# Pool group maps behind the keys' sums of squares in a two-layer hybrid decoder

## The chip, the cores and the metric

The kernel runs on one core of a Trainium2 chip. The metric is the device time of one execution in microseconds. The times of before are the median of three runs; the trace is one more execution, taken with the hardware profiler. TensorE (PE) multiplies matrices, VectorE (DVE) and ScalarE (ACT) do elementwise work, GpSimd (POOL) does some of it too, and SyncE (SP) issues most transfers. Each engine works through its own queue in order.

## What is computed

Two decoder layers over 264 token columns (256 of a prompt, 8 of a sample group), each of an FFN, a mixer and a second FFN, with a layer norm behind each. The mixer is a gated delta rule (four heads, from q, k, v) beside a causal pooling of four channel groups. Cut to what matters here:

```python
def pool_mix(p, buf, start_pos, pool_w, pool_scale):
    ...
    for gi, w in enumerate(POOL_WINDOWS):            # 2, 4, 8, 16
        s = end[:, :, sl] - cs[:, POOL_BUF + 1 - w:POOL_BUF + 1 - w + L, sl]
        means.append(s / cnt[None, :, None])
    d = jnp.concatenate(means, axis=-1) - ext[:, POOL_BUF:]
    y = jnp.einsum('blgc,gcd->blgd', d, pool_w).reshape(B, L, POOL_DIM) * pool_scale

def mixer(h, ...):
    proj = h @ w_in
    qkv_c, new_conv = causal_conv(qkv, conv_buf, conv_w)
    k = l2norm(k.reshape(B, L, DN_HEADS, DN_HEAD_DIM))
    ...
    out = jnp.concatenate([o_dn, o_pool], axis=-1) @ w_out
```

## The kernel before, in words

Activations lie transposed: 128 channels on the partitions, 264 tokens along the row. Every large product is done in three float32r matmuls: high part of the weight by high and by low part of the activation, and low part of the weight by the high part (`mm3`, lines 221 to 223). A product over 1024 channels is thus 24 matmuls into one PSUM tile.

Weights come from memory in units of two pieces. `W.load` issues the transfer into one of three `wraw` buffers, ScalarE rounds each piece into its high part (`whi`, line 180), and VectorE subtracts to get the low part (`wlo`, line 185); some pieces go to tiles named `xhi` and `xlo`. There are three pairs of `whi` and `wlo`, so a piece can be split once the product three places ahead of it is done. `W.ahead(n)` asks for pieces until `n` are ready or on their way.

TensorE's order is the order of the program. On the other engines a scheduler chooses the order when the kernel is built, by priority: what is written earlier comes first, and what stands inside `tc.high_priority()` goes ahead of it. After that the order is fixed.

In the mixer the products go q0, p3, q1, p2, q2, p1, q3, p0, v0 to v3, z0 to z3. `q_tile`, `v_tile` and the keys' `conv` (line 526) make a causal convolution: one ScalarE instruction and three on VectorE (128x255, 128x254, 128x253) into tiles `c0` to `c11`, of which `c0` to `c3` are the keys, `c4` to `c7` q and `c8` to `c11` v. `p_tile(g)` copies the product of Pool group g into `ext`, and GpSimd adds up windows there: g + 1 additions into `wsum` (line 615), of which two buffers exist; `ext` has two as well. `p_map(g)` does two things. At its call VectorE makes the difference `dm` of window mean and token, in four instructions (lines 626, 628, 630, 631); the function that it returns issues the map itself later: the matmul `py` (line 635), a scaled copy `yp` (line 637), and the split of `yp` into high and low part. For groups 0 to 2 the differences have raised priority, for group 3 not:

```python
                with tc.high_priority() if g < 3 else nullcontext():
                    nc.vector.scalar_tensor_tensor(dm[:, 16:SEQ], cur[:, 31:15 + SEQ], 1.0 / wd, ext[:, 31:15 + SEQ],
                                                   ALU.mult, ALU.subtract)
                    ...
                def finish():
                    py = psa.tile([P, T], F32, name="py", tag="ax")
                    nc.tensor.matmul(py, pw[:, g, :], dm, start=True, stop=True)
```

Beside these runs the gate: a chain of some 25 small VectorE instructions of 128x12 (`s_`, `y_`, `p_`, `xa`, `gg`) with raised priority. It ends in four products `gm` (line 708, 128x512 each), which `pdiff` (line 718) sums on TensorE into the decays `DT`. `sumsq` (lines 735 to 743) transposes the keys on TensorE (`psq`), squares them on ScalarE and adds them up on VectorE; with `wsc` that scales the scores `MT` (line 762), which are computed between the matmuls of v3. `pP` transposes `MT`, and the solver follows.

The FFN's last stage makes eight tiles `pd`. Ahead of the last two, weights for six pieces are asked for when another layer part follows (`xnext`), else for four.

Of the kernel before, what the change touches and what calls it, by code (L numbers as in the profile page):

```python
# [18 lines left out]
KD = D // P  # L19
# [71 lines left out]
def trunk(ctx: ExitStack, tc: tile.TileContext, a: dict):  # L91
# [28 lines left out]
    def behind(ins):  # L120
        return nullcontext() if ins is None else tc.issue_after(ins.ins)

    def tables(name):
        tc.keep_in_program_order(nc.scalar.preload_act_table_set(name))
# [9 lines left out]
    def split(hi, lo, src):  # L134
        ins = nc.scalar.activation(hi, src, AF.Copy)
        nc.vector.tensor_sub(lo, src, hi.bitcast(F32))
        return ins
# [79 lines left out]
    W = Weights(units)  # L217

    def mm3(ps, w, k, xh, xl, first, last):
        hi, lo = w  # L220
        nc.tensor.matmul(ps, hi[:, k, :], xh, start=first, stop=False)  # L221
        nc.tensor.matmul(ps, hi[:, k, :], xl, start=False, stop=False)  # L222
        nc.tensor.matmul(ps, lo[:, k, :], xh, start=False, stop=last)  # L223

    def product(w, nm):
        ps = psm.tile([P, T], F32, name="p" + nm, tag="mm")
        for k in range(KD):
            mm3(ps, w, k, HH[:, k, :], HL[:, k, :], k == 0, k == KD - 1)
        return ps

    def two_products(nms):

        ws = [W.get() for _ in nms]
        ps = [psm.tile([P, T], F32, name="p" + nm, tag="mm") for nm in nms]
        for k in range(KD):
            for p, w in zip(ps, ws):
                mm3(p, w, k, HH[:, k, :], HL[:, k, :], k == 0, k == KD - 1)
        return ps
# [190 lines left out]
    def ffn(src, norm, xnext, late=False):  # L429
        with tc.tile_pool(name="fp", bufs=1, reuse_waits="tile") as fp:  # L430
            gh = [fp.tile([P, T], F32R, name=f"gh{m}") for m in range(KF)]
            gl = [fp.tile([P, T], F32R, name=f"gl{m}") for m in range(KF)]

            def gate(m, y, bias, u, ubias):
                sg = fp.tile([P, T], F32, name="sg", tag="sg", bufs=2)
                gt = fp.tile([P, T], F32, name="gt", tag="gt", bufs=2)
                if bias is None:
                    with behind(hi1 if src is None and m == 0 else None):
                        nc.scalar.activation(sg, y, AF.Silu)
                    nc.vector.tensor_mul(gt, sg, u)  # L440
                else:
                    nc.scalar.activation(sg, y, AF.Silu, bias=bias)
                    nc.vector.scalar_tensor_tensor(gt, u, ubias, sg, ALU.add, ALU.mult)
                split(gh[m], gl[m], gt)

            first = 0
            if src is not None:
                W.ahead(6)
                raw = src.raw_products("gugugu", [((0,), 0, 6), ((1,), 0, 6), ((2,), 0, 6), ((3,), 0, 6), None,
                                                  ((0, 1, 2, 3), 6, KD), ((4, 5), 0, KD)] if late else  # L450
                                                 [((0, 1), 0, 4), None, ((0, 1), 4, KD), ((2, 3), 0, KD), ((4, 5), 0, KD)])
                src.normalise()
                W.after, W.after_hi = src.y_op, src.exp_op
                tables("silu_and_others")
                W.ahead(2)
                W.after = W.after_hi = None

                ws = [W.get(), W.get()]
                ps = [psa.tile([P, T], F32, name="p" + nm, tag="ax") for nm in "gu"]
                for k in range(KD):  # L460
                    for p, w in zip(ps, ws):
                        mm3(p, w, k, HH[:, k, :], HL[:, k, :], k == 0, k == KD - 1)
                W.ahead(2)
                for m in range(3):
                    gate(m, *src.settle(raw[2 * m]), *src.settle(raw[2 * m + 1]))
                gate(3, ps[0], None, ps[1], None)
                first = 4
            for m in range(first, KF):
                W.ahead(4)
                if src is None and m == 4:  # L470
                    constants_in()
                if src is None and m == 0:
                    pg, pu = two_products("gu")
                else:
                    pg = product(W.get(), "g")
                    pu = product(W.get(), "u")
                gate(m, pg, None, pu, None)
            tables("natural_log_exp_and_others")
            w, i = None, 0
            for m in range(KD):  # L480
                W.ahead(6 if m > 5 and xnext else 4)
                if m > 2:
                    norm.before(m, 2.0 * ALPHA)
                ps = psm.tile([P, T], F32, name="pd", tag="mm")
                for k in range(KF):
                    if i % KD == 0:
                        w = W.get()
                    mm3(ps, w, i % KD, gh[k], gl[k], k == 0, k == KF - 1)
                    i += 1
                    if m == 2 and k == 10:  # L490
                        norm.shift2()
                        norm.before(m, 2.0 * ALPHA)
                norm.add_scaled(m, ps, 2.0 * ALPHA)


    def mixer(l, src, norm, xstack):
        with tc.tile_pool(name="mp", bufs=1, reuse_waits="tile") as mp:
# [32 lines left out]
            def silu(after):  # L530
                for c in silus:
                    with tc.issue_after(after.ins):
                        nc.scalar.activation(c, c, AF.Silu)
                silus.clear()
# [42 lines left out]
            def q_tile(j, ps=None):  # L577
                W.ahead(4)
                conv(ps or product(W.get(), "q"), 4 + j)
                cq[j] = ct[4 + j]  # L580
# [39 lines left out]
            def p_map(g):  # L620
                ext, smp, cur = pend[g]
                wd = 2 << g
                dm = mp.tile([P, T], F32, name="dm", tag="dm", bufs=2)
                csm = cur[:, 15 + SEQ:].rearrange("p (b i) -> p b i", i=16)
                with tc.high_priority() if g < 3 else nullcontext():
                    nc.vector.scalar_tensor_tensor(dm[:, 16:SEQ], cur[:, 31:15 + SEQ], 1.0 / wd, ext[:, 31:15 + SEQ],
                                                   ALU.mult, ALU.subtract)
                    nc.vector.scalar_tensor_tensor(dm[:, SEQ:], csm[:, :, 15], 1.0 / wd, smp[:, :, 15],
                                                   ALU.mult, ALU.subtract)
                    nc.vector.tensor_mul(dm[:, 0:16], cur[:, 15:31], cst[:, C_INV + 16 * g:C_INV + 16 * g + 16])  # L630
                    nc.vector.tensor_sub(dm[:, 0:16], dm[:, 0:16], ext[:, 15:31])
# [4 lines that stand above are left out]
                    yp = lpool.tile([P, T], F32, name="yp", tag="sq", bufs=4)  # L636
                    nc.scalar.activation(yp, py, AF.Copy, scale=sm[:, l, S_PS + g:S_PS + g + 1])
                    split(mh[4 + g], ml[4 + g], yp)

                return finish  # L640
# [50 lines left out]
            conv(kr[3], 3)  # L691
            ck = ct[0:4]
            map3 = p_map(3)
            p_tile(1)
            map3()
            q_tile(3)
            map2 = p_map(2)
            p_tile(0)

# [19 lines left out]
                e_last = nc.scalar.activation(DT[:, :, j * P:(j + 1) * P], pd, AF.Exp)  # L719
            tables("silu_and_others")  # L720
            silu(e_last)
            map2()
            v_tile(0, e_last)
            map1 = p_map(1)


            ssa = mp.tile([P, 2 * H + 2 * H * NB], F32, name="ssa")
# [17 lines left out]
            v_tile(1, e_last)  # L745
            for t in range(2):
                sumsq(ck, ssk, ke, t)
            map1()
            v_tile(2, e_last)
            wsc = mp.tile([P, 2, H], F32, name="wsc")  # L750
            with tc.high_priority():
                nc.vector.reciprocal(wsc, ssk)
                nc.vector.tensor_mul(wsc, wsc, beta[:, 0:2, :])
            map0 = p_map(0)
            norm.centre()

# [535 lines left out]
    def constants_in():  # L1292
        nc.sync.dma_start(out=sm, in_=a["small"])
        nc.sync.dma_start(out=cst, in_=a["cst"])
        nc.scalar.activation(onr, cst[:, C_M1024:C_M1024 + P], AF.Copy)
        nc.scalar.activation(far, cst[:, C_ID:C_ID + P], AF.Copy, scale=-FAR)
        nc.scalar.activation(gto, cst[:, C_ONE:C_ONE + 2 * P].rearrange("p (i n) -> p i n", i=2), AF.Copy)
        for t in (*parts, kq.bitcast(F32)):
            nc.gpsimd.memset(t, 0.0)
# [105 lines left out]
```

## Time and profile before

| | us |
|---|---|
| median of three runs | 1093.57 (1092.8 to 1093.61) |
| the profiled execution | 1093.62 |
| its span, first to last instruction | 1091.8 |
| TensorE busy | 1050.5 (96%) |
| VectorE busy | 751.9 (69%) |
| ScalarE busy | 596.9 (55%) |
| GpSimd busy | 158.2 (14%) |

The chain that ended last is TensorE for 87% of the span, VectorE for 5%, "issue" for 3% and ScalarE for 3%. Busy shares are means over stages with different limits, so the stretch of a mixer in which TensorE waits is read by itself: the first layer's lies between 222 and 275 us of the span, the second layer's 535.8 us later. A time in brackets at a row's end is the idle time of the engine ahead of that instruction, with what ended it.

### The profile page before, as it was taken

What the parts mean: (1) busy time and instruction counts of PE and PEld (TensorE: products, weight loads), DVE (VectorE), ACT (ScalarE), POOL (GpSimd) and SP (SyncE); (2) the same over time, 40 slices, a digit from 0 to 9 for tenths busy, and PEclk for the clock granted to TensorE, in tenths of its full rate; (3) what the DMA queues carried; (4) which work ended last, traced back from release to release, by engine and by line L of the source; (5) the groups of instructions that cost most, each with busy time, mean ns of one, the idle gap of its engine ahead of it and who ended that gap; (6) DMA issues with size and microseconds to landing.
All of it is one profiled execution on the core that took longest, in us unless ns stands there. A gap on an engine that the chain in (4) does not pass through costs nothing.

```text
span 1091.8 us, 20807 instructions
## 1 busy us (share of the span) xinstructions
PE 1050.5 (96%) x8434; PEld 1033.1 (95%) x8434; DVE 751.9 (69%) x1223; ACT 596.9 (55%) x1081; POOL 158.2 (14%) x206
## 2 busy tenths in 40 slices
PE   8999999969999999999999999999699999999995
PEld 8999999959889999999999999999598999999995
DVE  5555567896789965557785555778787898555554
ACT  6444445647947744454574444466388377444443
POOL 0000022232540000003200000322233300000031
PEclk9999999989999999999999999999899999999998
DMA  8554445732234355544625545565331344554541
GB/s 305 186 192 175 176 177 185 278 122 89 81 135 163 139 192 194 182 168 190 242 101 198 177 175 191 180 238 190 111 113 64 133 187 157 191 184 171 187 155 40
DMA packets 35840, 183.23 MB, mean 168 GB/s; under 512 B 6817, under 2 KB 12577, under 8 KB 15521
## 3 DMA queue, kind: packets, MB, share of 16 engines
q1 hardware_dynamic: 28672, 175.19, 44.1%
q10 hardware_dynamic: 7072, 6.72, 1.8%
q8 instruction: 66, 1.08, 0.4%
q14 instruction: 30, 0.24, 0.1%
HBM read 175.18 MB, written 6.72 MB: 167 GB/s over the span
## 4 chain that ended last, share of the span: by engine, by line
PE 87%; DVE 5%; issue 3%; ACT 3%; DMA 2%; SPq 0%; ACTq 0%; DVEq 0%
PE pd L221 7%; PE pd L223 7%; PE pd L222 7%; PE pu L223 7%; PE pu L222 7%; PE pu L221 7%; PE pg L222 7%; PE pg L221 7%; PE pg L223 7%; ACT S L896 1%; DVE xlo L185 1%; PE pop L221 1%; DMA wba<-in_w_ba 1%; PE pq L221 1%; PE pq L222 1%
## 5 line engine op out<-in xcount | busy, mean ns | idle before, releaser
L185 DVE TENSOR_TENSOR wlo<-wraw,whi 128x1024 fp32r<-128x1024 f32 (+1 forms) x301 | 367.1, 1223 | 206.3 <-ACT whi L180 205.9
L180 ACT ACTIVATE whi<-wraw 128x1024 fp32r<-128x1024 f32 (+1 forms) x301 | 312.4, 1041 | 329.7 <-issue 116.9
L221 PE MATMUL pd<-gh,whi 128*128 128x264 f32 x704 | 200.3, 285 | 0.0
L223 PE MATMUL pd<-gh,wlo 128*128 128x264 f32 x704 | 199.9, 284 | 0.0
L222 PE MATMUL pd<-gl,whi 128*128 128x264 f32 x704 | 198.8, 282 | 0.0
L221 PE MATMUL pg<-HH,whi 128*128 128x264 f32 x632 | 179.6, 284 | 0.9 <-ACT whi L180 0.9
L222 PE MATMUL pg<-HL,whi 128*128 128x264 f32 x632 | 179.4, 284 | 0.7 <-DVE HL L381 0.7
L223 PE MATMUL pu<-HH,wlo 128*128 128x264 f32 x632 | 179.2, 284 | 0.8 <-DVE wlo L185 0.8
L223 PE MATMUL pg<-HH,wlo 128*128 128x264 f32 x632 | 179.4, 284 | 0.5 <-DVE wlo L185 0.5
L221 PE MATMUL pu<-HH,whi 128*128 128x264 f32 x632 | 179.4, 284 | 0.0
L222 PE MATMUL pu<-HL,whi 128*128 128x264 f32 x632 | 179.1, 283 | 0.0
L222 PEld LDWEIGHTS pd<-gl,whi 128*128 128x128 f32 x704 | 132.5, 188 | 0.0
L223 PEld LDWEIGHTS pd<-gh,wlo 128*128 128x128 f32 x704 | 132.5, 188 | 0.0
L221 PEld LDWEIGHTS pd<-gh,whi 128*128 128x128 f32 x704 | 132.5, 188 | 0.0
L222 PEld LDWEIGHTS pg<-HL,whi 128*128 128x128 f32 x632 | 119.2, 189 | 1.2 <-DVE HL L381 1.2
L221 PEld LDWEIGHTS pg<-HH,whi 128*128 128x128 f32 x632 | 119.1, 188 | 1.1 <-ACT whi L180 1.1
L223 PEld LDWEIGHTS pu<-HH,wlo 128*128 128x128 f32 x632 | 118.6, 188 | 1.2 <-DVE wlo L185 1.2
L223 PEld LDWEIGHTS pg<-HH,wlo 128*128 128x128 f32 x632 | 118.6, 188 | 0.8 <-DVE wlo L185 0.8
L222 PEld LDWEIGHTS pu<-HL,whi 128*128 128x128 f32 x632 | 119.2, 189 | 0.0
L221 PEld LDWEIGHTS pu<-HH,whi 128*128 128x128 f32 x632 | 119.2, 189 | 0.0
L305 POOL TENSOR_TENSOR s<-X 128x264 fp32r<-128x264 f32 x4 | 3.0, 761 | 632.2 <-DVE X L302 632.2
L440 DVE TENSOR_TENSOR gt<-sg,pu 128x264 f32<-128x264 f32 x79 | 33.9, 429 | 50.4 <-PE pu L223 50.4
(374 smaller groups left out, 2013.1 us busy)
## 6 DMA issues: line engine op xcount, KB each, us to landing
wraw<-in_f_gu SPq DMA_DIRECT2D x86, 1024.0 KB, 4.8
wraw<-in_f_d SPq DMA_DIRECT2D x44, 1024.0 KB, 4.8
wraw<-in_w_in SPq DMA_DIRECT2D x20, 1024.0 KB, 4.9
wraw<-in_w_out SPq DMA_DIRECT2D x8, 1024.0 KB, 4.8
S<-in_sdelta SPq DMA_DIRECT2D x8, 512.0 KB, 6.5
out_o_ds<-S ACTq DMA_DIRECT2D x8, 512.0 KB, 2.6
X<-in_xT ACTq DMA_DIRECT2D x4, 264.0 KB, 5.6
out_o_y<-X SPq DMA_DIRECT2D x4, 264.0 KB, 2.4
```

The source lines that it names most:

```text
L180: self.last_hi = nc.scalar.activation(h, r, AF.Copy)
L185: nc.vector.tensor_sub(l, r, h.bitcast(F32))
L221: nc.tensor.matmul(ps, hi[:, k, :], xh, start=first, stop=False)
L222: nc.tensor.matmul(ps, hi[:, k, :], xl, start=False, stop=False)
L223: nc.tensor.matmul(ps, lo[:, k, :], xh, start=False, stop=last)
L305: nc.gpsimd.tensor_add(self.s2, X[:, 0, :], X[:, 1, :])
L440: nc.vector.tensor_mul(gt, sg, u)
L896: nc.scalar.activation(s, s, AF.Copy, scale=ab[:, h * NB + b:h * NB + b + 1])
```

## The change

Three things are changed.

The maps of groups 3 and 2 are issued behind the keys' sums of squares, no longer behind `p_tile(1)` and ahead of v0; that of group 1 follows v2 and the scale `wsc`; the differences of group 1 are called with the map of group 2 done. Group 0's map stays behind v3. The differences of group 3 get raised priority like the others'. And in an FFN that another part follows, six pieces are asked for ahead of the seventh tile only; behind the last tile four are asked for.

```diff
-                W.ahead(6 if m > 5 and xnext else 4)
+                W.ahead(6 if m == 6 and xnext else 4)
...
                 norm.add_scaled(m, ps, 2.0 * ALPHA)
+                if m == KD - 1 and xnext:
+                    W.ahead(4)
...
-                with tc.high_priority() if g < 3 else nullcontext():
+                with tc.high_priority():
                     nc.vector.scalar_tensor_tensor(dm[:, 16:SEQ], cur[:, 31:15 + SEQ], 1.0 / wd, ext[:, 31:15 + SEQ],
...
             map3 = p_map(3)
             p_tile(1)
-            map3()
             q_tile(3)
             map2 = p_map(2)
             p_tile(0)
...
             silu(e_last)
-            map2()
             v_tile(0, e_last)
-            map1 = p_map(1)
...
             for t in range(2):
                 sumsq(ck, ssk, ke, t)
-            map1()
+            map3()
+            map2()
+            map1 = p_map(1)
             v_tile(2, e_last)
...
                 nc.vector.tensor_mul(wsc, wsc, beta[:, 0:2, :])
+            map1()
             map0 = p_map(0)
```

The third part moves nothing: with it or without it the rows on all five engines follow in the same order, and only numbers of tiles differ.

On TensorE, between the product p1 (`pp`) and the product q3 (`pq`) of the first mixer:

```order
 L222 MATMUL pp<-HL,whi 128x264
 L223 MATMUL pp<-HH,wlo 128x264
-L635 MATMUL py<-dm,pw 128x264
 L221 MATMUL pq<-HH,whi 128x264
 L222 MATMUL pq<-HL,whi 128x264
```

The map of group 3 no longer stands there; it and the map of group 2 come behind the eight transposes `psq`, ahead of v2.

On VectorE before, from the last step of the key tile `c1` (`c_2785`) over the low part of p1, the `wlo` (`c_2828` and `c_2875` are the key tiles c2 and c3, `c_2779` is q1's):

```order
L526 SCALAR_TENSOR_TENSOR c_2785<-raw,sm,c_2785 128x253
L662 TENSOR_TENSOR s__2714<-s__2714,e__2713 128x12
L526 SCALAR_TENSOR_TENSOR c_2828<-raw,sm,c_2828 128x255
L663 TENSOR_TENSOR y__2715<-s__2714 128x12
L526 SCALAR_TENSOR_TENSOR c_2875<-raw,sm,c_2875 128x255
L664 TENSOR_SCALAR p__2716<-y__2715 128x12
L185 TENSOR_TENSOR wlo<-wraw,whi 128x1024
L666 SCALAR_TENSOR_TENSOR p__2716<-p__2716,y__2715 128x12
L526 SCALAR_TENSOR_TENSOR c_2779<-pq,sm,c_2779 128x255
```

And VectorE now, in the same place:

```order
L528 SCALAR_TENSOR_TENSOR c_2785<-raw,sm,c_2785 128x253
L628 SCALAR_TENSOR_TENSOR dm<-wsum,ext 128x240
L630 SCALAR_TENSOR_TENSOR dm<-wsum,ext 128x8
L632 TENSOR_TENSOR dm<-wsum,cst 128x16
L664 TENSOR_TENSOR s__2714<-s__2714,e__2713 128x12
L528 SCALAR_TENSOR_TENSOR c_2828<-raw,sm,c_2828 128x255
L633 TENSOR_TENSOR dm<-dm,ext 128x16
L665 TENSOR_TENSOR y__2715<-s__2714 128x12
L185 TENSOR_TENSOR wlo<-wraw,whi 128x1024
L666 TENSOR_SCALAR p__2716<-y__2715 128x12
L528 SCALAR_TENSOR_TENSOR c_2779<-pq,sm,c_2779 128x255
```

The four differences of group 3 have come up to a place ahead of the small gate instructions, and the first step of c3 has gone behind. From there to the next `wlo`, that of q3, there stand five convolution steps among small `p_` instructions, before and now.

On VectorE before, from the low part of p0, the next `wlo` but one, to the second pair of `gm` (`c_2869` is q2's tile):

```order
L185 TENSOR_TENSOR wlo<-wraw,whi 128x1024
L708 TENSOR_TENSOR gm<-cst,gp 128x512 x2
L676 TENSOR_TENSOR gp<-gg,gp 128x8
L682 TENSOR_TENSOR ad<-as__2744,cst 8x32
L526 SCALAR_TENSOR_TENSOR c_2869<-pq,sm,c_2869 128x255
L708 TENSOR_TENSOR gm<-cst,gp 128x512 x2
```

And now, from the same `wlo` to the first pair of `gm`:

```order
L185 TENSOR_TENSOR wlo<-wraw,whi 128x1024
L671 SCALAR_TENSOR_TENSOR xa<-p__2716,xa 128x12
L528 SCALAR_TENSOR_TENSOR c_2869<-pq,sm,c_2869 128x255
L673 TENSOR_TENSOR gg<-xa,nega 128x12
L528 SCALAR_TENSOR_TENSOR c_2875<-raw,sm,c_2875 128x254
L528 SCALAR_TENSOR_TENSOR c_2869<-pq,sm,c_2869 128x254
L528 SCALAR_TENSOR_TENSOR c_2875<-raw,sm,c_2875 128x253
L709 TENSOR_TENSOR gm<-cst,gp 128x512 x2
```

Ahead of these rows, behind the low part of q3, the four differences of group 2 and the first step of c3 now stand; before, one difference of group 3 stood there, and the `gm` came straight behind p0's low part. One more step of q2's tile now stands between the two pairs of `gm`: four convolution steps more in all ahead of the second pair. On SyncE the loads of `ext` for groups 1 and 0 go from behind two weight loads to ahead of one each.

## Rows read from the trace of the kernel before

**Rows 1.** Waits of TensorE: engine, line, releaser; us in total, times, longest
```profile
PE py L635 <- issue: 21.1, 2, 10.6
```

**Rows 2.** Chain that ended last in time, first layer: start, us, what
```profile
234.45 10.56 issue
245.01 1.22 PE py L635 x2
...
253.33 2.28 PE pdiff L718 x10
255.61 0.45 PE py L635 x2
...
272.30 0.87 PE pP L1027 x8
```

**Rows 3.** Timeline of TensorE: start, us, engine, line, out<-in
```profile
222.68 0.28 PE L221 MATMUL pq<-HH,whi 128*128 128x264 f32 x1
...
225.58 0.28 PE L221 MATMUL pp<-HH,whi 128*128 128x264 f32 x1
...
245.66 0.79 PE L221 MATMUL pq<-HH,whi 128*128 128x264 f32 x1
...
253.17 0.62 PE L718 MATMUL pdiff<-gm,gto 128*128 128x512 f32 x2
```

**Rows 4.** Windows: length, busy PE, PEld, DVE, ACT, POOL, granted clock, DMA share, GB/s
```profile
203.00:206.00 3.00, 1.59 (x10) 1.34 (x10) 2.44 (x6) 0.92 (x4) 2.48 (x5) 1.00 1.06 388
...
240.00:242.00 2.00, 0.00 (x0) 0.00 (x0) 2.00 (x7) 0.00 (x0) 0.40 (x1) 0.50 0.63 266
```

**Rows 5.** Timeline of VectorE
```profile
227.11 0.81 DVE L662 TENSOR_TENSOR s__2714<-s__2714,e__2713 128x12 f32<-128x12 f32 x1
...
228.23 0.98 DVE L663 TENSOR_TENSOR y__2715<-s__2714 128x12 f32<-128x12 f32 x1
229.13 0.47 DVE L526 SCALAR_TENSOR_TENSOR c<-raw,sm,c 128x255 f32<-128x255 f32 x1
229.53 0.16 DVE L664 TENSOR_SCALAR p__2716<-y__2715 128x12 f32<-128x12 f32 x1
229.60 1.21 DVE L185 TENSOR_TENSOR wlo<-wraw,whi 128x1024 fp32r<-128x1024 f32 x1
230.74 0.81 DVE L666 SCALAR_TENSOR_TENSOR p__2716<-p__2716,y__2715 128x12 f32<-128x12 f32 x1
...
233.84 1.21 DVE L185 TENSOR_TENSOR wlo<-wraw,whi 128x1024 fp32r<-128x1024 f32 x1
...
238.84 1.27 DVE L708 TENSOR_TENSOR gm<-cst,gp 128x512 fp32r<-128x512 f32 x2
...
244.25 0.41 DVE L626 SCALAR_TENSOR_TENSOR dm<-wsum,ext 128x240 f32<-128x240 f32 x1 [1.66 <-POOL wsum L615]
...
244.74 0.17 DVE L631 TENSOR_TENSOR dm<-dm,ext 128x16 f32<-128x16 f32 x1
```

**Rows 6.** Timeline of GpSimd
```profile
225.87 3.32 POOL L615 TENSOR_TENSOR wsum<-wsum 128x396 f32<-128x396 f32 x3
230.09 1.43 POOL L615 TENSOR_TENSOR wsum<-ext 128x398 f32<-128x398 f32 x1 [0.91 <-POOL wsum L615]
241.60 2.62 POOL L615 TENSOR_TENSOR wsum<-wsum 128x396 f32<-128x396 f32 x2 [10.07 <-DVE dm L630]
...
247.76 0.85 POOL L615 TENSOR_TENSOR wsum<-ext 128x398 f32<-128x398 f32 x1 [2.00 <-ACT ext L609]
```

**Rows 7.** Timeline of SyncE's issues
```profile
230.84 6.65 SPq L162 DMA_DIRECT2D wraw<-in_w_in  x2
244.99 1.01 SPq L604 DMA_DIRECT2D ext<-in_spool  x2
```

**Rows 8.** Timeline of ScalarE
```profile
264.69 0.54 ACT L637 ACTIVATE yp<-py,sm 128x264 f32<-128x264 f32 x1
```

**Rows 9.** The page's DMA issues: KB each, median us to landing
```profile
wraw<-in_w_in SPq DMA_DIRECT2D x20, 1024.0 KB, 4.9
```

## The prediction

> **What bounds the kernel now.** I read the waits by engine first, for TensorE, because it is busy for 96% of the span. One line stands out: the matmul of a Pool group map, `py`, has TensorE idle for 21.1 us in two waits, one in each layer [rows 1]. The chain of waits, read in order of time, puts the first at 234.45 and makes it 10.56 us long; nothing else on that chain is near it [rows 2]. The chain calls its cause "issue", so I looked for it in the instructions in order of time on VectorE and GpSimd. `py` reads `dm`, and the last of the four instructions that fill the `dm` of group 3 is the 128x16 subtraction at 244.74 [rows 5]; `py` starts 0.1 us behind its end. In VectorE's queue that subtraction stands behind the first difference of group 2 (244.25), which had waited 1.66 us for GpSimd's sums. Those sums had themselves waited 10.07 us for VectorE, for a `wsum` buffer that group 3's differences still held [rows 6]. So the two engines wait for each other in turn, and the start of the loop is that group 3's differences, without priority, were drawn to the end of VectorE's backlog.
>
> The stall costs more than its length. In the windows, TensorE's granted clock is 1.00 over a stretch with an idle time of 1.4 us (203 to 206) and 0.50 in 240 to 242, that is 1.2 of 2.4 GHz, after TensorE had stood still for 5 us [rows 4]. A product of 24 matmuls takes 2.90 us at full clock (222.68 to 225.58); the two products behind the stall take 253.17 - 245.66 = 7.51 us, which is 1.71 us more than 5.80 [rows 3]. The two matmuls of `py` take 0.65 us there (245.01 to 245.66) against 0.45 at full clock: another 0.20 [rows 2, 3].
>
> **The change part by part.** *The maps.* On TensorE the map of group 3 leaves its place between the products p1 and q3, and the map of group 2 its place behind `pdiff`; both now stand behind `psq`, and the map of group 1 follows v2. None is added, so the eight matmuls per layer cost the same. The wait goes whole, since nothing that the new places read is late there: the differences of groups 3 and 2 are done some 15 us earlier. Taken away per layer: 10.56 + 1.71 + 0.20 = 12.47 us. That is the ceiling, 24.9 us for the two layers.
>
> *What is late next.* TensorE needs the low parts of weights, which VectorE makes, and VectorE had a backlog at 234: the low part of q3 was made at 233.84 to 235.05 [rows 5], already later than q3's third matmul could now run (234.45 + 0.24 = 234.7). So I walk VectorE's new order with the durations of before.
>
> Step 1: up to the end of the c1 step (227.11) nothing moves. Then group 3's differences come, and they wait for GpSimd, whose three sums end at 225.87 + 3.32 = 229.19; with VectorE idle the last two take nearer 0.85 than 1.1 each [rows 6], so about 228.9. A new wait of 1.8 us, behind which stand the small gate instructions, a convolution step and the low part of p1. The four differences take 0.57 us (244.25 to 244.74 and one more step) [rows 5]. But in that stretch before, two 128x12 instructions took 0.81 and 0.98 us instead of 0.16, because GpSimd was at work, and they end with its sums [rows 5, 6]. They now run behind the sums: 1.47 us less, start to start. One convolution step, 0.40 us (229.13 to 229.53), moves behind. The low part of p1 starts at 229.60 + 1.8 + 0.57 - 1.47 - 0.40 = 230.1 and ends at 231.3, just in time for p1 at 225.58 + 2 x 2.90 = 231.4.
>
> Step 2: from there to the low part of q3 it took 233.84 - 229.60 = 4.24 us, with one hold by GpSimd of 0.65 in it (230.74). Now GpSimd does all three sums of group 2 in this stretch, since no buffer is missing. The three holds that rows show (0.81, 0.98 and 0.81 against 0.16) cost 0.71 in the mean, so three cost 2.1 and the stretch takes 4.24 - 0.65 + 2.1 = 5.7. The low part of q3 starts at 235.8 and, 1.21 long, ends at 237.0 [rows 5]. **TensorE waits for it 2.3 us**; without holds it would be 0.2, with a full 0.85 for each 2.8.
>
> The Trainium skill ("SBUF — State Buffer", Who interferes with whom) says that a VectorE instruction with two inputs in SBUF and a GpSimd instruction that reads SBUF share a port as a lock, and the loser stands for the whole instruction. The long 128x12 rows agree, as they end when GpSimd does. By the rule taken strictly each of the five sums of groups 2 and 1 holds VectorE for its 0.85 us, 4.25 in place of the 2.85 that I take here and in step 3; that would put 2.8 us more on the two layers, 1079 us.
>
> Step 3: from the low part of q3 to the `gm` product that `pdiff` needs second, before: 238.84 + 0.61 - 233.84 = 5.61 us. Added in the new order: group 2's differences 0.57 for the 0.32 of one of group 3's, four convolution steps 1.58, a small instruction 0.08, and holds by the two sums of group 1 between 0 and 1.5, of which I take 0.75. That is 8.3 us: the `gm` is there at 244.1. TensorE, with its wait of 2.3, would be at this matmul at 234.45 + 5.80 + 0.23 + 2.3 = 242.8. **A second wait of 1.3 us.** Behind it VectorE makes v0's and v1's low parts (1.14 each) while `pdiff` needs 2.28 [rows 2], so no third wait; convolution and the SiLUs of the keys are done before `psq`.
>
> Step 4: behind `psq` two maps in place of one put two more ScalarE instructions (0.54 us for the first [rows 8]) and one VectorE instruction between the squares and the scale of the scores. TensorE also has one map more to do there, 0.45 us, which it does not do elsewhere; so only 0.3 us per layer is left as a wait. Nothing in the later order looks worse than that.
>
> *Priority* is what makes step 1 possible: alone it would end most of the stall. *The weight parts behind the last FFN tile:* the order on all five engines is the same with and without it, apart from tile numbers, so 0; the 1.4 us of idle at 203 stay [rows 4]. *On SyncE* two loads of `ext` move in front of weight loads; see the last rival.
>
> **Sum.** Per layer 12.47 - 2.3 - 1.3 - 0.3 = 8.6 us, for two layers 17.2. The profiled execution took 1093.62 us (1.8 outside its span), 0.05 over the median of the runs, so no correction: 1093.6 - 17.2 = 1076.4; I say 1076. A change of 0.2%, 2 us, is about the least that a measurement of this kernel can tell.
>
> **Rivals.** *A, the holds do not come:* VectorE and GpSimd slip past each other. Step 2 then leaves 0.2 us and step 3 0.6, so 11.6 per layer, 1070. For it: convolution steps of 0.47 us stand between held rows, not held themselves. Against: every 128x12 instruction that met a running sum was held. 17%.
>
> *B, the queue runs later and the clock falls:* full holds of 0.85 give waits of 2.8 us at q3 and 2.0 at `pdiff`, and with 0.6 behind `psq` 7.1 per layer are left, 1079.4; if TensorE falls to 0.50 in them, 1.71 per layer is lost again: 1083. Against the clock part: it held 1.00 over the idle 1.4 us, and these are two waits with a product between them. The Trainium skill ("TensorE: Matmul & The Clock Gate", HAM oscillation) says that idle gaps send the clock back to half; no row here shows a gap of 2 to 3 us. 17%.
>
> *C, another wait takes the stall's whole place:* the maps leave, but VectorE's queue holds TensorE as long at q3 and `pdiff`, so within 2 us of 1093. For it: VectorE stood idle for only 1.66 us in the whole stall [rows 5], so its backlog is real. Against: it would have to hold TensorE for 12.5 us, and the waits that I can name, with full holds, come to 5.4. 3%.
>
> *D, slower:* SyncE. The load of v2's and v3's weights was issued at 230.84 [rows 7]. Now it stands behind an `ext` load that waits for group 3's last difference and the store of its tail (the two such loads of before were issued at 244.99, just behind those differences). In the walk that is 230, and the buffer for the weights comes free at 231.3, so nothing is lost. v2 starts at about 254 (`pdiff`, two products, `psq` and two maps behind 244.1); less 4.9 us to land [rows 9] and 2.3 to split, the load must be issued by 246.8. Beyond that each microsecond is lost, and only past 255.4 would a layer be slower than before. At 260, for example, that is 4.6 per layer, 1103. 2%.
>
> **How the numbers follow.** Forecast 60% (1073 to 1079.5), A 17%, B 17%, C 3%, D 2%, the rest beyond. A range of 1070 to 1082 takes in A's value, both ends of the holds and the first half of B, and leaves out some 15%. Faster by over 0.2% is the forecast with A and B and a part of C: 95%; within 0.2%: 2%; slower: 3%.
>
> **What would show it.** In the new profile: no wait of TensorE before `py`, clock 1.00 from 234 to 256. Step 1 is right if VectorE waits some 2 us for `wsum` before the first `dm`. Step 2: TensorE waits about 2 us for `wlo` at the third matmul of q3, 30 us behind the idle time at 203 to 206. Step 3: about 1.3 us before the second `pdiff` matmul, released by `gm`. Step 4: `pP` 8 to 9 us earlier than 272.30 [rows 2]. The forecast is wrong if long `wlo` waits come at v0 to v2, or if the idle at 203 changes.

## The result, and the profile after

The changed kernel takes **1076.4 us** for 1093.6, ratio 0.984 (95% interval 0.982 to 0.986). Its profiled execution took 1076.49 us, with a span of 1074.7. One of its four executions, at a mean granted clock of 0.588, took 1623.86 us and does not count in the ratio; the other three lie between 1076.03 and 1076.49. 1076 was predicted, in a range of 1070 to 1082.

First the waits of TensorE, which answer to [rows 1]: us in total, times, longest.

```profile
PE pq L223 <- DVE wlo L185: 4.2, 2, 2.1
PE ps L346 <- DVE acc L285: 3.1, 2, 1.7
...
PE pdiff L719 <- DVE gm L709: 1.3, 1, 1.3
```

The 21.1 us ahead of `py` are gone. In their place stands a wait of 2.1 us in both layers at q3's third matmul, for its low part, and one of 1.3 us at `pdiff`, but in one layer only. The timeline of VectorE in the first layer shows why they are there (answers to [rows 5]; in brackets the idle time ahead):

```profile
229.25 0.41 DVE L628 SCALAR_TENSOR_TENSOR dm<-wsum,ext 128x240 f32<-128x240 f32 x1 [1.82 <-POOL wsum L617]
...
230.41 1.22 DVE L185 TENSOR_TENSOR wlo<-wraw,whi 128x1024 fp32r<-128x1024 f32 x1
231.55 0.85 DVE L666 TENSOR_SCALAR p__2716<-y__2715 128x12 f32<-128x12 f32 x1
...
232.71 0.61 DVE L668 SCALAR_TENSOR_TENSOR p__2716<-p__2716,y__2715 128x12 f32<-128x12 f32 x1
...
233.64 0.80 DVE L668 SCALAR_TENSOR_TENSOR p__2716<-p__2716,y__2715 128x12 f32<-128x12 f32 x1
...
235.78 1.21 DVE L185 TENSOR_TENSOR wlo<-wraw,whi 128x1024 fp32r<-128x1024 f32 x1
...
242.12 0.82 DVE L678 TENSOR_TENSOR gp<-gg,gp 128x8 f32<-128x8 f32 x1
...
243.36 1.63 DVE L709 TENSOR_TENSOR gm<-cst,gp 128x512 fp32r<-128x512 f32 x2
```

VectorE waits 1.82 us for GpSimd's sums of group 3, makes p1's low part, and then three small instructions take 0.85, 0.61 and 0.80 us where 0.16 is usual. They end within 0.03 us of GpSimd's three sums of group 2 (232.38, 233.29 and 234.41), which answer to [rows 6]; I call such a lengthening a hold. q3's low part comes at 235.78.

```profile
230.60 1.78 POOL L617 TENSOR_TENSOR wsum<-ext 128x398 f32<-128x398 f32 x1
232.45 1.96 POOL L617 TENSOR_TENSOR wsum<-wsum 128x396 f32<-128x396 f32 x2
```

The two layers are not alike behind that wait. TensorE in the first and in the second layer, with the idle time in brackets:

```profile
237.05 0.39 PE L223 MATMUL pq<-HH,wlo 128*128 128x264 f32 x1 [2.12 <-DVE wlo L185]
...
244.26 0.69 PE L719 MATMUL pdiff<-gm,gto 128*128 128x512 f32 x2
...
764.14 0.39 PE L223 MATMUL pq<-HH,wlo 128*128 128x264 f32 x1 [2.09 <-DVE wlo L185]
...
769.83 0.40 PE L719 MATMUL pdiff<-gm,gto 128*128 128x512 f32 x1
771.53 0.50 PE L719 MATMUL pdiff<-gm,gto 128*128 128x512 f32 x1 [1.31 <-DVE gm L709]
```

And windows of both layers: length, busy time of PE, PEld, DVE, ACT, POOL, then the granted clock, DMA share, GB/s.

```profile
238.00:240.00 2.00, 2.00 (x12) 2.00 (x11) 2.00 (x7) 0.16 (x2) 0.11 (x1) 0.55 0.15 41
240.00:242.00 2.00, 2.00 (x12) 2.00 (x12) 2.00 (x5) 1.34 (x5) 1.39 (x1) 0.60 0.72 213
...
766.00:768.00 2.00, 2.00 (x18) 2.00 (x18) 2.00 (x7) 0.65 (x5) 0.30 (x1) 1.00 0.54 86
768.00:770.00 2.00, 2.00 (x18) 1.90 (x16) 2.00 (x5) 1.57 (x4) 2.00 (x1) 1.00 0.85 352
```

In the first layer the granted clock is 0.55 and 0.60 behind the idle time of 2.12 us, so mostly 1.2 of 2.4 GHz; in the second it holds 1.00 behind one of 2.09. To compare layers and kernels I count from the first matmul of `pba`, the small product that feeds a mixer's gate (before 214.43 and 750.24; after 214.68 and 741.80). The first `pdiff` matmul starts 29.58 us behind it in the first layer and 28.03 in the second: the slow clock cost 1.55 us. But the end of `pdiff` is the same, 32.09 and 32.06 us from that matmul. What the clock lost, the wait for `gm` would have taken anyway. The distance of the two mixers is 527.12 us for 535.81, 8.69 less.

### The profile page after: what moved, and what is told of

It reads as the page before. It is cut to its first block, busy times and chain, and to the rows that moved or that the text cites. A ratio compares the mean times of both kernels' runs of the same rounds, so it can differ in the third digit from the quotient of the medians.

```text
span 1074.7 us, 20803 instructions
## 1 busy us (share of the span) xinstructions
PE 1049.0 (98%) x8434; PEld 1031.1 (96%) x8434; DVE 752.9 (70%) x1223; ACT 596.8 (56%) x1081; POOL 155.3 (14%) x206
## 4 chain that ended last, share of the span: by engine, by line
PE 87%; DVE 7%; DMA 2%; issue 2%; ACT 1%; POOL 1%; ACTq 0%; SPq 0%; DVEq 0%; POOLq 0%
PE pd L221 8%; PE pd L223 7%; PE pd L222 7%; PE pu L223 7%; PE pu L222 7%; PE pu L221 7%; PE pg L222 7%; PE pg L221 7%; PE pg L223 7%; DVE wlo L185 1%; DVE xlo L185 1%; PE pop L221 1%; PE pP L1041 1%; POOL wsum L617 1%; PE pout L222 1%
```

## The experiments

All are timed beside the kernel before on the same chip, where that took 1093.6 to 1094.5 us; so rows are compared by the ratio, or by distances. The waits are idle times of TensorE, and the last three columns are distances from a mixer's first `pba` matmul to the end of `pdiff` and to the first matmul of `psq` and of `pP`, all in us from the timeline of TensorE; two values are the two layers.

| kernel | us | ratio to before (95%) | wait at q3 | at `pdiff` | `pdiff` ends | `psq` starts | `pP` starts |
|---|---|---|---|---|---|---|---|
| before | 1093.6 | | 0 (`py` 10.6) | 0 | 41.2 | 47.3 | 57.7 |
| after | 1076.4 | 0.984 | 2.1 | 0 / 1.3 | 32.1 | 37.8 | 49.1 |
| FFN part alone | 1093.4 | 0.999 (0.997–1.000) | 0 (`py` 10.6) | 0 | 41.5 | 47.6 | 58.0 |
| priority alone | 1081.2 | 0.988 (0.987–0.990) | 1.7 | 2.9 | 35.3 / 35.5 | 41.4 / 42.6 | 51.8 / 53.0 |
| maps alone | 1079.8 | 0.987 (0.985–0.988) | 0.4 | 0 | 28.8 | 36.4 | 49.8 / 49.5 |
| no sums of group 2 | 1072.7 | 0.980 (0.979–0.982) | 0.9 | 0.8 | 30.3 | 36.0 | 47.3 |
| sums of group 2 twice | 1080.7 | 0.988 (0.986–0.990) | 3.7 | 0 | 33.9 | 39.5 | 50.9 |
| q3's low part first | 1079.2 | 0.986 (0.984–0.988) | 1.2 | 2.1 | 33.5 | 39.9 | 51.2 |
| maps, three `ext` | 1081.0 | 0.988 (0.986–0.989) | 0.4 | 0 | 28.8 | 36.7 | 50.7 / 49.4 |
| late differences | 1073.6 | 0.981 (0.979–0.983) | 0.4 | 0 | 28.8 | 35.4 | 46.7 / 47.3 |
| after, again | 1076.4 | 0.984 (0.982–0.985) | 2.1 | 1.3 / 0 | 32.1 | 37.8 | 49.1 |
| late, with FFN part | 1073.5 | 0.981 (0.980–0.982) | 0.4 | 0 | 28.8 | 35.4 | 46.7 / 47.1 |

**The three parts, each alone.** *The FFN part:*

```diff
-                W.ahead(6 if m > 5 and xnext else 4)
+                W.ahead(6 if m == 6 and xnext else 4)
...
+                if m == KD - 1 and xnext:
+                    W.ahead(4)
```

> The kernel before with only the third part of the change: in an FFN that another part follows, six weight pieces are asked for ahead of the seventh tile, and four behind the last. Theory: no row moves on any engine, so 1093.6 us within 0.2%, and the 10.56 us wait ahead of py stays in both layers. Rival: this part has a share in the gain, by another placing of the tiles; then some of the 17 us comes here.

1093.36 us, no difference that can be told, and the wait of before in full (waits of TensorE):

```profile
PE py L636 <- issue: 21.2, 2, 10.6
```

*The raised priority:*

```diff
-                with tc.high_priority() if g < 3 else nullcontext():
+                with tc.high_priority():
```

> The kernel before with only the raised priority for the differences of group 3; the maps stay where they were. Theory of the prediction (priority alone ends most of the stall): the wait of 10.56 us ahead of py goes, VectorE waits 1.8 us for wsum and TensorE 2.1 us at q3 as after the whole change; but the differences of group 1 now stand between the two pairs of gm and wait for GpSimd's sums, which end at 243.85 after the whole change, so the second pair comes about 1.2 us later than there: 1.2 per layer, 1079 us. Rival: the new places of the maps carry the gain, and priority alone leaves over half of it behind: 1085 or more.

1081.2: 13.0 us of the 17 come from this part alone. The wait at q3 is 1.7 us for the 2.1 expected, because the map (0.45 us) still stands ahead of q3 here. The mechanism at `pdiff` is the expected one. VectorE, with priority alone, in the first layer:

```profile
243.49 0.41 DVE L626 SCALAR_TENSOR_TENSOR dm<-wsum,ext 128x240 f32<-128x240 f32 x1 [1.67 <-POOL wsum L615]
...
244.92 1.27 DVE L708 TENSOR_TENSOR gm<-cst,gp 128x512 fp32r<-128x512 f32 x2
```

The second pair of `gm` waits for group 1's differences, TensorE waits 2.90 us at `pdiff`, and its second matmul there starts 31.35 us from the mixer's start (29.73 in the second layer after the change), 1.6 later for the 1.2 expected. What I had not counted is the clock: behind this wait it is 0.50 in 246 to 248 (in the second layer in 776 to 780), and `pdiff` ends 3.2 us later, not 1.6.

*The maps:* the hunks of the change from `map3()` to `map0 = p_map(0)`.

> The kernel before with only the maps moved; the differences of group 3 keep their low priority. VectorE's order is the one before up to the low part of q3, so it makes that at 233.84 to 235.05 and TensorE waits 0.35 us at q3, not 2.1; the second gm is there at 239.5, before TensorE gets to pdiff, so no wait there; GpSimd does group 2's last two sums only after 241. Theory A: the stall is py's place alone; without the raised priority 12.47 - 0.35 - 0.3 = 11.8 per layer are gained, 1070 us, 6 us less than with the whole change, and the raised priority costs what maps alone would give. Theory B (the prediction's sentence that priority is what makes it possible): the late differences hold ext and wsum, ScalarE stands at the copy of p1 until 245, and v1 (which takes p1's PSUM tile) or the keys' SiLUs ahead of psq wait for it; then 2 to 6 us per layer come back, 1075 to 1083.

Up to `pdiff` theory A holds: a wait of 0.4 us at q3, none at `pdiff`, which ends at 28.8 for 32.1 after the whole change. Behind it theory B takes most of this back (waits of TensorE, then ScalarE and VectorE):

```profile
PE pz L223 <- DVE wlo L185: 5.2, 2, 2.6
PE pv L221 <- ACT ext L609: 3.4, 2, 1.7
...
PE psq L733 <- ACT c L533: 1.9, 4, 0.8
```

```profile
245.11 0.39 ACT L607 ACTIVATE ext<-pp 128x256 f32<-128x256 f32 x1 [5.56 <-POOL wsum L615]
```

```profile
244.86 0.17 DVE L631 TENSOR_TENSOR dm<-dm,ext 128x16 f32<-128x16 f32 x1
```

The row of ScalarE names GpSimd's sums, but those had ended at 244.33. The copy of p1 starts 0.08 us behind group 3's last difference, which holds the `ext` buffer; v1 waits for the PSUM tile that the copy reads, and the keys' SiLUs come late. The wait of 2.6 us at z0 stands in neither theory: z0's low part stands behind the solver's first steps in VectorE's queue (266.76). Behind it the clock fell to 0.50 in the first layer (268 to 270) and not in the second, and from `pP` to the first `pop`, the mixer's output product, it takes 31.1 and 29.7 us for 28.3 after the whole change.

So either part alone ends most of the stall (13.0 and 14.4 us), and they don't add, since it is the same stall; together they gain 17.2.

**Is it GpSimd that holds VectorE?** The window sums of group 2 left out, then done twice:

```diff
-                for s in range(g + 1):
+                for s in range(0 if g == 2 else g + 1):
...
-                    nc.gpsimd.tensor_add(nx[:, lo + d:], cur[:, lo + d:], cur[:, lo:EXT - d])
+                    for _ in range(2 if g == 2 else 1):
+                        nc.gpsimd.tensor_add(nx[:, lo + d:], cur[:, lo + d:], cur[:, lo:EXT - d])
```

> The kernel after, with GpSimd's three window sums of group 2 left out (its differences read the tokens themselves, so the output of that group is another one). Step 2 of the prediction: those sums hold three small gate instructions of VectorE, by 0.69, 0.45 and 0.64 us in the trace after. Without them the differences of group 2 stand 0.57 us ahead of q3's low part, so TensorE's wait at q3 should go from 2.1 to 2.1 - 1.78 + 0.57 = 0.9 us, the second gm come 1.8 us earlier, and the time be 1076.4 - 2 x 1.8 = 1072.8. Rival: the low part is late because of the length of VectorE's queue, and the long rows only show waiting that would be there anyway: q3's wait 2 us or more, 1076 to 1077.

1072.65 and a wait of 0.9 us at q3, both as expected. VectorE without the sums has the same small instructions at 0.17:

```profile
231.29 0.17 DVE L666 TENSOR_SCALAR p__2716<-y__2715 128x12 f32<-128x12 f32 x1
...
231.76 0.16 DVE L668 SCALAR_TENSOR_TENSOR p__2716<-p__2716,y__2715 128x12 f32<-128x12 f32 x1
```

> The kernel after, with each of GpSimd's three window sums of group 2 done twice (the same sum into the same place). The counterpart of the run without them, which gave 1072.65 us with a wait of 0.9 us at q3. Theory: six sums hold all six small gate instructions ahead of q3's low part, three more by 0.6 us each: q3's wait goes from 2.1 to 3.9, the second gm comes 1.8 to 1.9 us later, the time is 1076.4 + 2 x 1.9 = 1080.2. Rival: VectorE is held only by the first sums after a change of buffers, the others slip past: under 1 us per layer, 1077 to 1078.

1080.67, a wait of 3.7. All six small instructions are held (0.86, 0.62, 0.81, 0.61, 0.80 and 0.60 us); the later three:

```profile
234.47 0.61 DVE L669 SCALAR_TENSOR_TENSOR p__2716<-p__2716,y__2715 128x12 f32<-128x12 f32 x1
...
235.40 0.80 DVE L669 SCALAR_TENSOR_TENSOR p__2716<-p__2716,y__2715 128x12 f32<-128x12 f32 x1
...
236.51 0.60 DVE L669 SCALAR_TENSOR_TENSOR p__2716<-p__2716,y__2715 128x12 f32<-128x12 f32 x1
```

That GpSimd's sums cause the holds is shown, in both directions. The clock falls behind q3's longer wait in both layers here (0.63 and 0.51 in 238 to 242, 0.50 in 768 to 770); `pdiff` does not wait, and ends at 33.9 in both.

**Does q3's wait count by itself?** Its low part is brought forward, and nothing else:

```diff
             def q_tile(j, ps=None):
+                W.rush = j == 2
                 W.ahead(4)
+                W.rush = False
...
-                            with behind(after):
+                            with behind(after), tc.high_priority() if self.rush else nullcontext():
                                 nc.vector.tensor_sub(l, r, h.bitcast(F32))
```

> The kernel after, with the weight's low parts that are asked for ahead of q2 at raised priority. One thing moves on VectorE: q3's low part goes ahead of two convolution steps and two small gate instructions, 0.95 us of work, and what stands ahead of the gm is the same work in another order. Theory A (one chain, VectorE's, up to the second gm sets where pdiff ends): TensorE's wait at q3 falls from 2.1 to 1.2 us, its wait at pdiff grows by the same, and the time stays 1076.4 within 0.1%. If TensorE's clock, which was 0.55 to 0.60 behind the wait of 2.1 us in one layer, then stays at 1.00, that too is worth nothing. Theory B (each wait counts by itself, as the sum of the prediction has it): 0.9 per layer are gained, and 1.6 more where the clock stays up: 1073 to 1074.6.

1079.2 beside a before of 1094.5: nothing gained, and the mixers stand 529.3 us apart for 527.1. Waits of TensorE, the rows at `pdiff`, and a window behind it:

```profile
PE pdiff L722 <- DVE gm L712: 4.7, 4, 2.1
...
PE pq L224 <- DVE wlo L186: 2.3, 2, 1.2
```

```profile
243.89 0.50 PE L722 MATMUL pdiff<-gm,gto 128*128 128x512 f32 x1 [2.05 <-DVE gm L712]
...
245.15 2.00 PE L722 MATMUL pdiff<-gm,gto 128*128 128x512 f32 x5 [0.30 <-DVE gm L712]
```

```profile
246.00:248.00 2.00, 2.00 (x7) 1.62 (x7) 2.00 (x4) 0.98 (x2) 0.00 (x0) 0.50 0.03 4
```

The second `pdiff` matmul stands 29.77 us from the mixer's start, for 29.73 after: theory A's one chain, to 0.04 us. What 0.9 us less at q3 give, `pdiff` takes. But the clock now falls behind the wait at `pdiff`, in both layers, where no later wait covers it. With another 0.3 us at a `gm` that GpSimd held (the second pair takes 2.29 us for 1.63), `psq` starts 2.1 us later. Theory A's "the time stays" was wrong for that reason, and theory B's gain did not come at all.

**What the late differences hold.** The maps alone, with a third buffer for `ext`:

```diff
-                ext = mp.tile([P, EXT], F32, name="ext", tag="ext", bufs=2)
+                ext = mp.tile([P, EXT], F32, name="ext", tag="ext", bufs=3)
```

> The maps moved and nothing else (1079.8 us), with a third buffer for ext. In the run with two, ScalarE stood at the copy of p1 into ext until group 3's late differences let the buffer go (245.1), TensorE waited 1.7 us at v1 for it, 0.8 and more at psq for the keys' SiLUs, and 2.6 at z0 for a low part that stood behind the solver's first steps. Theory: the copy of p1 no longer waits, so the 1.7 us at v1 goes; the copy of p0 still waits for group 3's buffer, with the decays' exponentials and the SiLUs behind it, so psq starts no earlier than 252.5, about where it starts after the whole change; the low part of z0 stands ahead of the solver in this order, so the 2.6 us goes: 1076, as the whole change. Rival: the late differences have no cost through ext, and the waits stay: 1079 to 1080.

1080.97, a miss: 1076 was expected, and it is no better than with two buffers. The waits of 1.7 at v1 and 2.6 at z0 are gone (0.4 and 0.5 are left), but TensorE gets to `psq` sooner and waits there, up to 1.5 us at a time. ScalarE:

```profile
245.29 0.39 ACT L607 ACTIVATE ext<-pp 128x256 f32<-128x256 f32 x1 [3.81 <-DVE dm L631]
...
248.63 1.28 ACT L124 ACT_TABLE_LOAD   x1
249.93 2.56 ACT L533 ACTIVATE c<-c 128x256 f32<-128x256 f32 x8
```

The copy of p0 holds the decays and the SiLUs, as expected; that the waits at `psq` would grow by what was saved at v1 I had not walked. And the clock is 0.50 in 252 to 254 of the first layer.

**A version that beats the whole change.** From those readings: let `gm` go first. Group 3's differences wait for the last `gm`, group 2's follow v0, and `ext` has three buffers.

```diff
-            map3 = p_map(3)
             p_tile(1)
...
-            map2 = p_map(2)
...
+            map3 = p_map(3, g_last)
...
             v_tile(0, e_last)
+            map2 = p_map(2, g_last, False)
```

`p_map`'s new arguments put its differences behind that instruction, the second time without raised priority; `g_last` is the last `gm`.

> A version meant to beat the kernel after: maps moved, three ext buffers, group 3's differences with raised priority but held back until the last gm is issued, group 2's behind v0 without priority. GpSimd then does only one sum of group 2 ahead of the gm, and no difference stands ahead of the low parts of q3 and p0. Theory: q3's wait 0.35 us, the second gm at 239, no wait at pdiff, so TensorE is at pdiff 3.6 us earlier than after the whole change (240.65 for 244.26); the copy of p0 waits until about 243.3 for group 3's ext, the SiLUs end at 249, psq waits 0.3 to 0.5: 3.1 to 3.3 per layer, 1070. Rival: the exponentials behind the copy of p0 hold psq, or the sums that now run beside v0 and v1 hold their low parts: a gain of under 1 us per layer, 1075 or more.

> The kernel after once more, on the same chip as the next run, so that the two can be compared. Theory: 8.7 us per layer less than before (the distance from the first mixer's first product to the second's was 527.1 us for 535.8), 1076 to 1077; TensorE waits 2.1 us at q3 in both layers, and where the clock falls behind that wait, pdiff starts later and ends at the same distance from the mixer's start, 32.1 us. Rival: the clock's fall costs its 1.6 us; then an execution with falls in other places has another distance, 525.5 or 528.7.

> The version with group 3's differences held back behind the last gm, group 2's behind v0 and three ext buffers (1073.63 us beside a before of 1094.48), now with the third part of the change too, so that it differs from the kernel after in this alone. Theory: the same order of rows, so the distance of the mixers is 525.3 us, 1.8 less than after, and in the second layer about the same again: 3 to 3.6 us less than the kernel after on the same chip, ratio to before 0.981. Rival: the gain over after was the chip's; then the two are within 1 us.

1073.6, and with the FFN part 1073.5 beside 1076.4 for the kernel after on the same chip (1072.8 to 1073.6 for 1075.7 to 1077.3): 2.9 us less, a little under the 3 to 3.6 expected for the pair. The 1070 expected for the first run was a miss. TensorE in the last of these:

```profile
235.23 0.39 PE L223 MATMUL pq<-HH,wlo 128*128 128x264 f32 x1 [0.43 <-DVE wlo L185]
...
240.90 0.62 PE L717 MATMUL pdiff<-gm,gto 128*128 128x512 f32 x2
...
244.25 0.39 PE L223 MATMUL pv<-HH,wlo 128*128 128x264 f32 x1 [0.67 <-DVE wlo L185]
```

`pdiff` ends 3.3 us earlier than after the change, `psq` starts 2.4 earlier: v0 now waits 0.67 us for its low part, which stands behind group 3's differences and is lengthened beside GpSimd's sums (v0's and v1's take 3.25 us for 2.34). Behind `pP` a further 0.6 us per layer is lost (28.8 us to the first `pop` for 28.3), whose cause I did not follow.

In the second execution of the kernel after, the fall of the clock came in the other layer: `pdiff` starts at 28.02 and 29.57 and ends at 32.07 and 32.08. Its mixers stand 527.9 us apart, 0.7 of which is a longer idle time at the second one's norm (2.11 for 1.42).

## Why the prediction was right

**Steps 1 to 4, per layer** (in us; measured in the second layer, where the clock holds 1.00).

| term | predicted | measured |
|---|---|---|
| stall, its slow clock and `py` go | 12.47 | 12.7 |
| VectorE waits for `wsum` | 1.8 | 1.82 |
| lost at q3 | 2.3 | 2.38 (idle 2.09) |
| lost at `pdiff` | 1.3 | 1.58 (idle 1.31; in the first layer the slow clock takes its place) |
| lost behind `psq` | 0.3 | 0 |
| `pP` earlier | 8.6 | 8.64 and 8.63 (both layers) |

The measured losses are taken from starts. q3's first matmul stood 31.22 us from the mixer's first `pba` matmul and stands at 19.85; 0.45 of that is `py`, and the two products behind it took 7.57 us for 5.80: together 12.7. After the change it is 8.18 us from q3's first matmul (761.65) to the first of `pdiff` (769.83), for the 5.80, and 4.03 us from there to the end of `pdiff`, for 2.45 before. Each loss is some 0.3 us more than the idle time, without the sums of group 2 too (1.16 for 0.89 at q3): a matmul's row lasts 0.28 us, but the next one starts 0.12 behind it, and behind a wait 0.23. 12.7 - 2.4 - 1.6 is 8.7, within 0.1 of the distance measured. The order on VectorE, walked through with durations of the trace, gave the two waits, and their prices to within 0.3 us, before any run.

**Sizes that were off.** The three holds of step 2 were priced at 0.71 each and measured 0.69, 0.45 and 0.64, 1.78 in all for 2.1. The holds of step 3 were taken as 0.75 and came to 1.0: `gp` 0.82 for 0.15, and the second pair of `gm` 1.63 for 1.27 [rows 5]. The two errors nearly cancel, which is luck. The Trainium skill ("SBUF — State Buffer", Who interferes with whom) would have the loser stand for the whole other instruction; the trace agrees that one engine holds the other, at a mean price of 0.59 us beside sums of 0.84 to 1.0 us. That VectorE meets a sum already under way, as the second held instruction does (it starts at 232.71, in a sum of 232.45 to 233.29), would fit this; it wasn't tried by itself.

**Two steps failed** inside the right sum. *Step 4* expected a wait of 0.3 us behind `psq` and one map more on TensorE there. There is no wait: TensorE is busy without a gap from `psq` to `pP` (252.42 to 263.75), and what grew is the work. Before, two maps stood in that stretch; after, all four do (TensorE before, then after):

```profile
262.56 0.61 PE L635 MATMUL py<-dm,pw 128*128 128x264 f32 x2
...
271.69 0.61 PE L635 MATMUL py<-dm,pw 128*128 128x264 f32 x2
```

```profile
253.28 1.06 PE L637 MATMUL py<-dm,pw 128*128 128x264 f32 x4
...
257.08 0.60 PE L637 MATMUL py<-dm,pw 128*128 128x264 f32 x2
...
263.31 0.60 PE L637 MATMUL py<-dm,pw 128*128 128x264 f32 x2
```

From `psq` to `pP` it takes 11.34 us for 10.45, and the 0.89 more are the maps of groups 3 and 2, which left earlier places and cost nothing in sum. So the 0.3 was too much here, about as much as the price of the wait at `pdiff` was too little; that the sum came out at 8.6 owes something to luck.

The other is *the clock*, in the forecast's "clock 1.00 from 234 to 256" and in the argument against rival B. One idle time of 1.4 us that kept the clock [rows 4] was no evidence for one of 2.1: the clock fell in one layer of each of two executions. The Trainium skill ("TensorE: Matmul & The Clock Gate", HAM oscillation) tells of idle gaps, longer ones than these, that send it back to half; here the shorter ones did, and not each time. The forecast held all the same, because of something that it did not say: the two waits are not two prices, but two places on one chain. VectorE's queue, from p1's low part to the second pair of `gm`, sets where `pdiff` ends, and TensorE has 1.3 us to spare between q3 and there. The chain of waits shows it in the second layer, where it goes past q3 on VectorE alone:

```profile
762.95 1.13 DVE wlo L185
765.21 1.14 DVE wlo L185
...
770.45 1.04 DVE gm L709
771.53 2.32 PE pdiff L719 x9
```

q3's low part brought forward then showed that a fall of the clock does cost time where no later wait covers it.

**"Priority alone would end most of the stall"** was right (13.0 us), and said too little: the maps alone end as much.

**The rivals.** A's missing holds came only where the sums were left out. Its value leaves out the 0.3 us of step 4 (with them 11.4 per layer, 1071), and both readings that were weighed for and against it are too strong: in the trace of before a small reciprocal (226.12, 0.22 us as without a sum) passed beside a running sum, and a convolution step behind it (226.26) took 0.92 us for 0.47. B's waits were too long, and its fall of the clock cost nothing in this order. C and D did not come; SyncE's load of `ext` goes out at 230.49 and the load of weights behind it 1.2 us later, as walked ([rows 7]):

```profile
230.49 0.33 SPq L606 DMA_DIRECT2D ext<-in_spool  x1
231.66 0.33 SPq L162 DMA_DIRECT2D wraw<-in_w_in  x1
```

One sign moved a little: the idle time at 203, ahead of the norm's `ps`, is 1.73 us in the first layer for 1.41, and 1.42 in the second. With the maps alone and no FFN part it was 1.66 and 1.41, with the FFN part alone 1.41 twice; what moves it is open.

## What to carry to other kernels

When a stall of one engine on another goes, walk the other engine's queue in its new order, with durations of the trace: the next waits can be named and sized before a run. Then ask which of them sets the end, since two waits on one queue are one price, and an idle time with a later wait to cover it can lose the clock for nothing, while one of like length without such cover pays for the slow clock too. Two cures of one stall don't add, and each alone may leave buffers held that the other sets free.

## What was not expected of the hardware

An idle time of 2.1 us ahead of the same matmul lowered the granted clock in one of two layers, in either one (2.12 and 2.10 with a fall, 2.09 and 2.11 without). One of 2.11 ahead of a norm's `ps` (the kernel after, again) did not lower it, one of 2.05 ahead of `pdiff` (q3's low part first) did in both layers, and so did 2.90 and 3.7. Even 1.47 ahead of `psq`, with a wait of 0.28 half a microsecond behind it, was followed by 0.50 in the first layer of the maps with three `ext`, while 1.70 at v1 in the maps alone was not. Waits of 0.9 and 0.8 us, some 6 us apart, lowered it in neither layer. Small VectorE instructions beside GpSimd's sums took 0.6 to 0.86 us for 0.16, one for each of group 2's sums, with three sums as with six; most convolution steps between them kept their 0.47.
